# Projections with both halves of the input in one matmul, norms transposed and evicted by token tile

## The chip, the cores and the metric

The kernel runs on one core of a Trainium2 chip. The core has a matrix engine (TensorE, PE), a vector engine (VectorE, DVE), a scalar engine (ScalarE, ACT), GpSimd (POOL) and a queue engine (SyncE, SP) that issues most transfers. PE writes into PSUM, of which the kernel holds 8 banks of 128 partitions x 512 f32. The engines run their own instruction streams in order and meet by semaphores. The metric is device microseconds of one execution; the median of several runs counts.

## The reference, cut to what matters

One decoder layer for 256 tokens of width 1024, all in float32. It mixes tokens in two attention branches, then runs an expert FFN.

```
xn = rms_norm(h, norm_mix_g)
[qa ka va | qb kb vb | f_logit | g_a g_b] = xn @ w_in
ya = moba_attention(rope(qa), rope(ka), va) @ w_branch_a     # 8 heads of 64; one block: plain causal
yb = forgetting_attention(qb, kb, vb, log_sigmoid(f_logit + b)) @ w_branch_b   # 8 heads of 64
h  = h + (sigmoid(g_a) * ya + sigmoid(g_b) * yb) @ w_out
h  = h + peer_ffn(rms_norm(h, norm_ffn_g), ...)              # 8 product-key heads, top 16, 16384 experts
return rms_norm(h, norm_final_g)
```

In the forgetting attention (FoX) each score gets the difference of two cumulated logs of forget gates added: a column term for the query and a row term for the key.

## The kernel before, in words

To keep float32 accuracy every large product is made of three in a faster form: a factor is split into a high half (its value rounded to that form) and a low half (the rest), and `hi*hi + hi*lo + lo*hi` is added up in PSUM. `split` (L78) does this for a weight: SP loads a 128x1024 piece (512 KB) into one of three `raw` buffers, ACT casts the high half (L82), DVE subtracts (L83). `mm3` (L91) issues the three matmuls, L92, L95 and L96.

A projection (`proj_t`, L166) multiplies one such weight piece with the normed, transposed input `xt`: eight pieces of the contraction (`KD = 8`), three matmuls of 128x256 each, so 24. `xt1` (first norm) and `xt2` (second norm) are pairs of tiles, high and low. The first projections of a norm are "late": the 16 matmuls with the high weight come first (L176) and the 8 with the low one last (L178).

`norm_t` (L138) makes such an input. For the two token tiles it computes the scale (squares L126, root L133, reciprocal L135), scales on DVE (`xn`, L145), transposes 16 blocks on PE into four banks (L151) and evicts eight 128x256 tiles, each first on ACT (high half, L156) and then on DVE (low half, L157).

The order in the program: the first norm; the forget gate's logits (24 small matmuls) and their chain of log-sigmoid, cumulated sum and negation (L218 to L230); a small array goes to memory (`cd`) and comes back broadcast to all partitions (`crow`, L234, on POOL's queue); eight FoX projections for q and k, four value pieces (`w_va`); FoX attention woven with the eight MoBA projections, MoBA attention woven with the 16 gate projections; then branch and output projections, the second norm, 16 `w_pq` projections of the FFN, and 2 x 128 expert pieces. On each engine the framework's scheduler fixes the order when the program is built; `after` adds orders by hand. PSUM has four names (`tp`, `sp`, `py`, `mm`) of two banks each. 14 matmuls on zeros (L199) run while the input is loaded.

Of the kernel before, what the change touches and what calls it, by code (L numbers as in the profile page):

```python
# [50 lines left out]
def body(ctx, tc, x, g_mix, w_fb, w_va, w_qk, w_gate, w_f, b_f, w_br, w_out, g_ffn, w_pq,  # L51
# [24 lines left out]
    lows = []  # L76

    def split(src, behind=None):  # L78
# [3 lines left out]
        ih = nc.scalar.copy(out=h, in_=r)  # L82
        il = nc.vector.tensor_tensor(out=l, in0=r, in1=h.bitcast(F32), op=ALU.subtract)  # L83
        lows.append(il)
        if behind is not None:
            for i, b in zip((ih, il), behind):
                if b is not None:
                    after(i, b)
        return h, l

# [14 lines left out]
    xt2 = [keep.tile([P, KD, S], F32R, name=f"xt2{i}") for i in "hl"]  # L105
# [32 lines left out]
    def norm_t(pool, xin, gi, xt, tags, junk, vector=(), cuts=(512, 1024)):  # L138
        xs = []
        for t in range(NT):  # L140
            rs = norm_rstd(pool, xin[:, t], junk, vector[t] if vector else (), cuts)
            xn = pool.tile([P, D], F32, name="xn", bufs=2)
            for n in range(2):
                sl = slice(n * 512, (n + 1) * 512)
                nc.vector.tensor_scalar(out=xn[:, sl], in0=xin[:, t, sl], scalar1=rs, scalar2=None, op0=ALU.mult)  # L145
            xs.append(xn)
        pss = [bank(tag) for tag in tags]
        for t in range(NT):
            for k in range(KD):
                o = (k % 2 * NT + t) * P  # L150
                nc.tensor.transpose(pss[k // 2][:, o:o + P], xs[t][:, k * P:(k + 1) * P], ident)  # L151
        evs = []
        for k in range(KD):
            g = gm[:, gi, k:k + 1]
            src = pss[k // 2][:, k % 2 * S:(k % 2 + 1) * S]
            ia = nc.scalar.mul(out=xt[0][:, k], in_=src, mul=g)  # L156
            iv = nc.vector.scalar_tensor_tensor(  # L157
                out=xt[1][:, k], in0=src, scalar=g, in1=xt[0][:, k].bitcast(F32),
                op0=ALU.mult, op1=ALU.subtract)
            evs.append(ia)  # L160
        return ia, iv, evs[1]
# [4 lines left out]
    def proj_t(src, xt, behind=None, tag="mm", late=False):  # L166
        w = split(src, behind)
        ps = bank(tag)[:, :S]
        if not late:
            for k in range(KD):  # L170
                mm3(ps, wk(w, k), [v[:, k] for v in xt], k == 0, k == KD - 1)
        else:

            for k in range(KD):
                for v in xt:
                    nc.tensor.matmul(ps, lhsT=wk(w, k)[0], rhs=v[:, k], start=k == 0 and v is xt[0], stop=False)  # L176
            for k in range(KD):
                nc.tensor.matmul(ps, lhsT=wk(w, k)[1], rhs=xt[0][:, k], start=False, stop=k == KD - 1)  # L178
# [3 lines left out]
    with ExitStack() as fr:  # L182
# [15 lines left out]
        for _ in range(14):  # L198
# [9 lines left out]
        xt1 = [fp.tile([P, KD, S], F32R, name=f"xt1{i}") for i in "hl"]  # L208
# [5 lines left out]
        ps = bank("tp")[:HEADS, :S]  # L214
        for k in range(KD):
            mm3(ps, wk(wfs, k, HEADS), [v[:, k] for v in xt1], k == 0, k == KD - 1)
        fx = fp.tile([HEADS, S], F32, name="fx")
        nc.vector.tensor_scalar(out=fx, in0=ps, scalar1=bf, scalar2=None, op0=ALU.add)  # L218
        fa = fp.tile([HEADS, S], F32, name="fa")
        nc.scalar.activation(out=fa, in_=fx, func=AF.Abs)  # L220
        nc.scalar.activation(out=fa, in_=fa, func=AF.Exp, scale=-1.0)
        nc.scalar.activation(out=fa, in_=fa, func=AF.Ln, bias=1.0)
        lf = fp.tile([HEADS, S], F32, name="lf")
        nc.vector.scalar_tensor_tensor(out=lf, in0=fx, scalar=0.0, in1=fa, op0=ALU.min, op1=ALU.subtract)
        cf = fp.tile([HEADS, S], F32, name="cf")
        nc.vector.tensor_tensor_scan(out=cf, data0=lf, data1=lf, initial=0.0, op0=ALU.add, op1=ALU.bypass)

        cn = fp.tile([HEADS, 3 * P], F32, name="cn")
        nc.vector.tensor_scalar(out=cn[:, P:], in0=cf, scalar1=-1.0, scalar2=None, op0=ALU.mult)
        nc.vector.tensor_scalar(out=cn[:, :P], in0=cf[:, :P], scalar1=-1.0, scalar2=None, op0=ALU.mult)  # L230
        cd = drm.tile([HEADS, 3 * P], F32, name="cd")
        nc.gpsimd.dma_start(out=cd, in_=cn)
        crow = fp.tile([P, HEADS, 3, P], F32, name="crow")
        nc.gpsimd.dma_start(out=crow.rearrange("p h t k -> p (h t k)"), in_=cd.rearrange("h k -> (h k)").partition_broadcast(P))  # L234

        cq = fp.tile([P, NT, HEADS], F32, name="cq")
        tp = bank("tp")
        for t in range(NT):
            nc.tensor.transpose(tp[:, t * HEADS:(t + 1) * HEADS], cf[:, t * P:(t + 1) * P], ident[:HEADS, :HEADS])
        nc.scalar.copy(out=cq, in_=tp[:, :NT * HEADS].rearrange("p (t h) -> p t h", h=HEADS))  # L240

        mask = cmx[:, C_MASK:C_MASK + 3 * P]
        def heads_qk(br, i):
            fox = br == 0
            dst = []
            for c in range(4):
                behind = (normed1[2] if c == 0 else normed1[0], normed1[1]) if fox and i == 0 and c < FIRST else None
                ps = proj_t((w_fb if fox else w_qk)[i * 4 + c], xt1, behind, late=behind is not None, tag=("mm", "sp", "mm", "py")[c] if fox else "mm")
                q = fp.tile([P, S], F32, name=f"qk{br}{i}{c}")
                sc = 0.125 if i == 0 else 1.0  # L250
                if fox:
                    nc.scalar.mul(out=q, in_=ps, mul=sc)
                else:
                    q0 = fw.tile([P, S], F32, name="q0")
                    nc.scalar.mul(out=q0, in_=ps, mul=sc)
                    qp = [fw.tile([P, S], F32R, name=f"q0{i}") for i in "hl"]
                    nc.scalar.mul(out=qp[0], in_=ps, mul=sc)
# [11 lines left out]

        def projections(br, res):  # L270
            res.append((yield from heads_qk(br, 0)))
            res.append((yield from heads_qk(br, 1)))
            if br == 0:
# [5 lines left out]
            for c in range(4):  # L279
                w = split(w_va[br * 4 + c])  # L280
                for t in range(NT):
                    for kk in range(2):
                        k = 2 * c + kk
                        mm3(pv[t], [a[:, k, t * P:(t + 1) * P] for a in xt1], wk(w, kk, 512), k == 0, k == KD - 1)
# [5 lines left out]
        def attention(br, qs, ks, v):  # L290
# [7 lines left out]
            if fox:  # L298
                for hh in (slice(0, 4), slice(4, 8)):
                    nc.vector.tensor_tensor(out=crow[:, hh, 0::2], in0=crow[:, hh, 0::2], in1=mask[:, :P].unsqueeze(1).unsqueeze(1).to_broadcast([P, 4, 2, P]), op=ALU.add)  # L300
            for h in range(HEADS + 1):
                if h < HEADS:
# [6 lines left out]
                    if fox:  # L309
                        ch = crow[:, h].rearrange("p t k -> p (t k)")  # L310
                        for t, o, n in ((0, 0, P), (1, P, S)):
                            nc.vector.scalar_tensor_tensor(out=s[:, o:o + n], in0=sp[:, o:o + n], scalar=cq[:, t, h:h + 1], in1=ch[:, o:o + n], op0=ALU.add, op1=ALU.add)
# [67 lines left out]
        mt = [fp.tile([P, KD, S], F32R, name=f"xt1{i}") for i in "hl"]  # L380
# [25 lines left out]
        def w_out_step(k, t, n, behind=None):  # L406
            ps, lo, hi = po[t][n]
            return mm3(ps[:, :hi - lo], [a[:, k, t * P:(t + 1) * P] for a in mt], [a[:, lo:hi] for a in ws[k]], k == 0, k == KD - 1, behind)
# [8 lines left out]
        for t in range(NT):  # L417
            for n, (ps, lo, hi) in enumerate(po[t]):
                for k in range(KD - LATE, KD):
                    last = w_out_step(k, t, n, last)  # L420
                nc.vector.tensor_tensor(out=x2[:, t, lo:hi], in0=ps[:, :hi - lo], in1=xin[:, t, lo:hi], op=ALU.add)
# [363 lines left out]
```

## Time and profile before

| | |
|---|---|
| runs | 1024.62, 1026.22 (median), 1028.5 us |
| profiled execution | 1024.9 us, span 1023.1 us from first to last instruction |
| mean granted clock of PE | 0.996 of full speed |
| busy | PE 98%, weight loads 90%, DVE 73%, ACT 53%, POOL 1% of the span |
| memory | 176.88 MB read, 174 GB/s over the span |

The first 55 us hold the norm and the FoX projections, the second norm lies near 210 us, and the FFN takes the remaining 800 us; busy shares of the whole are mostly those of the FFN.

### The profile page before, as it was taken

The numbers are of one execution on the slowest core, as the hardware profiler recorded it, in microseconds if no ns is written. First come the engines' busy times: TensorE is split into PE (matmuls) and PEld (weight loads), VectorE is DVE, ScalarE is ACT, GpSimd is POOL, SyncE is SP. The second block draws the span as 40 slices with busy tenths as digits, with TensorE's granted clock in tenths as the row PEclk, the third lists the DMA queues.
The fourth block names the chain that finished last, engine by engine and source line by source line (L and its number), as shares of the span: only waits on it lengthen the run. The fifth ranks groups of instructions, "written<-read, shape, count | busy, mean of one in ns | idle before, by whom it ended". The sixth has DMA issues, their size and how long they took to land.

```text
span 1023.1 us, 18580 instructions
## 1 busy us (share of the span) xinstructions
PE 1007.5 (98%) x7068; PEld 924.6 (90%) x7068; DVE 748.6 (73%) x1603; ACT 541.9 (53%) x983; POOL 7.4 (1%) x13
## 2 busy tenths in 40 slices
PE   8999999989999999999999999999999999999997
PEld 6898999989999999999999999988888888888886
DVE  5575546679999996788888889866656666665665
ACT  6555566454554544555544444455555555555554
POOL 0000000000000000000000000000000000000001
PEclk9999999999999999999999999999999999999999
DMA  6654435655566565555555555566566666666663
GB/s 217 221 154 130 127 110 182 186 167 164 149 190 200 173 186 178 165 163 164 159 164 163 162 164 165 166 185 196 195 190 198 189 192 197 191 197 190 193 197 123
DMA packets 50040, 179.14 MB, mean 175 GB/s; under 512 B 5768, under 2 KB 6672, under 8 KB 49696
## 3 DMA queue, kind: packets, MB, share of 16 engines
q1 hardware_dynamic: 49104, 175.62, 55.9%
q0 software_dynamic: 416, 1.69, 0.5%
q8 instruction: 55, 0.90, 0.4%
q10 hardware_dynamic: 432, 0.66, 0.2%
q14 instruction: 33, 0.27, 0.1%
HBM read 176.88 MB, written 1.06 MB: 174 GB/s over the span
## 4 chain that ended last, share of the span: by engine, by line
PE 97%; DVE 1%; DMA 0%; ACT 0%; issue 0%; SPq 0%; DVEq 0%; ACTq 0%
PE mm L92 17%; PE mm L95 17%; PE mm L96 17%; PE py L92 7%; PE py L95 7%; PE py L96 7%; PE sp L96 6%; PE sp L95 6%; PE sp L92 6%; PE tp L608 3%; PE mm L176 1%; PE sp L308 1%; PE sp L577 1%; PE tp L324 1%; PE mm L178 0%; DMA xin<-in_x_dram 0%
## 5 line engine op out<-in xcount | busy, mean ns | idle before, releaser
L83 DVE TENSOR_TENSOR lo<-raw,hi 128x1024 fp32r<-128x1024 f32 x328 | 399.8, 1221 | 134.7 <-ACT hi L82 134.7
L82 ACT CAST hi<-raw 128x1024 fp32r<-128x1024 f32 x328 | 344.8, 1053 | 281.2 <-PE mm L95 181.9
L92 PE MATMUL mm<-xt2h,hi 128*128 128x256 f32 x1128 | 323.6, 287 | 0.0
L96 PE MATMUL mm<-xt2h,lo 128*128 128x256 f32 x1128 | 317.2, 281 | 0.0
L95 PE MATMUL mm<-xt2l,hi 128*128 128x256 f32 x1128 | 317.0, 281 | 0.0
L92 PEld LDWEIGHTS mm<-xt2h,hi 128*128 128x128 f32 x1128 | 212.5, 188 | 0.3
L95 PEld LDWEIGHTS mm<-xt2l,hi 128*128 128x128 f32 x1128 | 212.7, 189 | 0.0
L96 PEld LDWEIGHTS mm<-xt2h,lo 128*128 128x128 f32 x1128 | 212.5, 188 | 0.0
L645 ACT CAST ah<-act 128x256 fp32r<-128x256 f32 x128 | 52.0, 407 | 95.1 <-PE sp L95 95.1
L646 DVE TENSOR_TENSOR al<-act,ah 128x256 fp32r<-128x256 f32 x128 | 54.3, 425 | 61.5 <-PE sp L96 60.5
L95 PE MATMUL py<-lo,ah 128*128 128x512 f32 x256 | 79.8, 389 | 0.0
L92 PE MATMUL py<-hi,ah 128*128 128x512 f32 x256 | 79.7, 389 | 0.0
L96 PE MATMUL py<-hi,al 128*128 128x512 f32 x256 | 79.4, 389 | 0.0
L95 PE MATMUL sp<-lo,ah 128*128 128x512 f32 x254 | 79.0, 389 | 0.0
L92 PE MATMUL sp<-hi,ah 128*128 128x512 f32 x254 | 78.8, 389 | 0.0
L96 PE MATMUL sp<-hi,al 128*128 128x512 f32 x254 | 78.7, 389 | 0.0
L602 DVE TENSOR_TENSOR oh<-iota,slot_e 128x512 f16<-128x512 f16 x128 | 53.5, 420 | 21.8 <-PE tp L608 21.1
L92 PE MATMUL mm<-xt1h,hi 128*128 128x256 f32 x208 | 60.3, 290 | 0.0
L96 PE MATMUL mm<-xt1h,lo 128*128 128x256 f32 x208 | 59.5, 286 | 0.0
L95 PE MATMUL mm<-xt1l,hi 128*128 128x256 f32 x208 | 59.2, 285 | 0.0
L96 PEld LDWEIGHTS py<-hi,al 128*128 128x128 f32 x256 | 48.1, 188 | 10.0
L92 PEld LDWEIGHTS py<-hi,ah 128*128 128x128 f32 x256 | 48.1, 188 | 10.0
(256 smaller groups left out, 1333.6 us busy)
## 6 DMA issues: line engine op xcount, KB each, us to landing
raw<-in_u_t_dram SPq DMA_DIRECT2D x128, 512.0 KB, 3.6
raw<-in_v_e_dram SPq DMA_DIRECT2D x128, 512.0 KB, 3.6
raw<-in_w_gate_dram SPq DMA_DIRECT2D x16, 512.0 KB, 3.6
raw<-in_w_pq_dram SPq DMA_DIRECT2D x16, 512.0 KB, 3.9
raw<-in_w_fb_dram SPq DMA_DIRECT2D x8, 512.0 KB, 4.1
raw<-in_w_va_dram SPq DMA_DIRECT2D x8, 512.0 KB, 3.7
raw<-in_w_qk_dram SPq DMA_DIRECT2D x8, 512.0 KB, 3.7
raw<-in_w_br_dram SPq DMA_DIRECT2D x8, 512.0 KB, 3.6
```

What stands on the lines that cost most here:

```text
L82: ih = nc.scalar.copy(out=h, in_=r)
L83: il = nc.vector.tensor_tensor(out=l, in0=r, in1=h.bitcast(F32), op=ALU.subtract)
L92: i = nc.tensor.matmul(ps, lhsT=lhs[0], rhs=rhs[0], start=start, stop=False)
L95: nc.tensor.matmul(ps, lhsT=lhs[0], rhs=rhs[1], start=False, stop=False)
L96: return nc.tensor.matmul(ps, lhsT=lhs[1], rhs=rhs[0], start=False, stop=stop)
L176: nc.tensor.matmul(ps, lhsT=wk(w, k)[0], rhs=v[:, k], start=k == 0 and v is xt[0], stop=False)
L308: nc.tensor.matmul(sp[:, o:o + n], lhsT=q[:, t * P:(t + 1) * P], rhs=k[:, :n], start=True, stop=True)
L324: nc.tensor.transpose(tp[:, j * P:(j + 1) * P], pg[:, j * P:(j + 1) * P], ident)
L602: nc.vector.tensor_tensor(out=oh, in0=iota.unsqueeze(1).to_broadcast(wide), in1=slot_e[:, :, s2].unsqueeze(2).to_broadcast(wide), op=ALU.i ...
L608: nc.tensor.matmul(ps[:, q * NK:(q + 1) * NK], lhsT=ohs[q // 2][:, 1, :, q % 2], rhs=gis[q // 2][:, part, :, q % 2], start=part == 0, stop ...
L645: nc.scalar.copy(out=ah, in_=at(i))
L646: nc.vector.tensor_tensor(out=al, in0=at(i), in1=ah.bitcast(F32), op=ALU.subtract)
```

## The change

Four things change. First, `xt` becomes one tile in which the high and low half of a piece lie side by side, so that one matmul of 512 columns multiplies both with a high weight; `proj_w` does so for 7 FoX, 8 MoBA and 16 gate projections, and the two halves of the result are added when evicted (`both`: ACT copies one, DVE adds the other). The scale of 0.125 goes from the eviction into `split`. Second, both norms are transposed and evicted token tile by token tile, in 128x128 blocks; a tile's blocks lie in two banks. Third, the first projection of each norm starts with tile 0 (`mm2_t`), and the forget gate's matmuls stand behind its first eight. The forget chain comes after the fourth FoX projection, its broadcast array has 256 instead of 384 values a head, and its columns are transposed after the eighth projection. Fourth, there are 22 matmuls on zeros for 14. The order of the loads on SP's queue stays. The other `w_pq` projections, the expert pieces, branch and output projections stay as they were.

```diff
+    def split(src, behind=None, scale=None):
...
+            ih = nc.scalar.mul(out=h, in_=r, mul=scale)
+            il = nc.vector.scalar_tensor_tensor(out=l, in0=r, scalar=scale, in1=h.bitcast(F32), op0=ALU.mult, op1=ALU.subtract)
...
+    def mm2(ps, w, xt, then=None, ks=range(KD)):
+        for k in ks:
+            i = nc.tensor.matmul(ps, lhsT=wk(w, k)[0], rhs=xt[2][:, k], start=k == 0, stop=False)
...
+        for k in ks:
+            i = nc.tensor.matmul(ps[:, :S], lhsT=wk(w, k)[1], rhs=xt[0][:, k], start=False, stop=k == KD - 1)
+    def mm2_t(ps, w, xt, t, then=None):
+        for k in range(KD):
+            i = nc.tensor.matmul(ps[:, t * S:(t + 1) * S], lhsT=wk(w, k)[0], rhs=xt[2][:, k, :, t * P:(t + 1) * P], start=k == 0 and t == 0, stop=False)
...
+    def both(out, ps):
+        nc.scalar.copy(out=out, in_=ps[:, S:])
+        return nc.vector.tensor_tensor(out=out, in0=ps[:, :S], in1=out, op=ALU.add)
...
-    xt2 = [keep.tile([P, KD, S], F32R, name=f"xt2{i}") for i in "hl"]
+    xt2 = parts(keep.tile([P, KD, 2, S], F32R, name="xt2"))
...
-                o = (k % 2 * NT + t) * P
-                nc.tensor.transpose(pss[k // 2][:, o:o + P], xs[t][:, k * P:(k + 1) * P], ident)
+            blocks = [pss[2 * t + k % 2][:, k // 2 * P:(k // 2 + 1) * P] for k in range(KD)]
...
+                ia = nc.scalar.mul(out=xt[0][:, k, cols], in_=blocks[k], mul=g)
+                iv = nc.vector.scalar_tensor_tensor(
+                    out=xt[1][:, k, cols], in0=blocks[k], scalar=g, in1=xt[0][:, k, cols].bitcast(F32),
+                    op0=ALU.mult, op1=ALU.subtract)
...
-        for _ in range(14):
+        for _ in range(22):
...
+        w0 = split(w_fb[0], (normed1[2], normed1[1]), 0.125)
+        ps0 = bank("mm")
+        first0 = mm2_t(ps0, w0, xt1, 0)
...
+            gate_last = mm3(ps, wk(wfs, k, HEADS), [v[:, k] for v in xt1[:2]], k == 0, k == KD - 1, first0 if k == 0 else None)
...
-        crow = fp.tile([P, HEADS, 3, P], F32, name="crow")
+        crow = fp.tile([P, HEADS, S], F32, name="crow")
...
             res.append((yield from heads_qk(br, 0)))
+            if br == 0:
+                forget()
...
-                ps = proj_t(w_gate[c], xt1)
-                g = gate[:, c // KD, c % KD]
-                nc.scalar.copy(out=g, in_=ps)
+                ps = proj_w(w_gate[c], xt1)
+                both(gate[:, c // KD, c % KD], ps)
```

The first place is ACT's stream at the start of the program, from the first eviction of the first norm to the forget gate's Abs (`fa`). `hi<-raw` are high halves of weight pieces, `tp`, `sp`, `py` are banks. Before:

```order
L156 ACTIVATE xt1h<-tp,gm 128x256
L156 ACTIVATE xt1h<-sp,gm 128x256
L156 ACTIVATE xt1h<-tp,gm 128x256
L156 ACTIVATE xt1h<-py,gm 128x256
L156 ACTIVATE xt1h<-tp,gm 128x256
L82 CAST hi<-raw 128x1024
L156 ACTIVATE xt1h<-sp,gm 128x256
L156 ACTIVATE xt1h<-tp,gm 128x256
L156 ACTIVATE xt1h<-py,gm 128x256
L82 CAST hi<-raw 128x1024 x3
L220 ACTIVATE fa<-fx 8x256
```

And of the change, from the sixth block on:

```order
L206 ACTIVATE xt_130<-sp,gm 128x128
L206 ACTIVATE xt_130<-tp,gm 128x128 x2
L206 ACTIVATE xt_130<-py,gm 128x128
L206 ACTIVATE xt_130<-sp,gm 128x128
L206 ACTIVATE xt_130<-tp,gm 128x128 x2
L206 ACTIVATE xt_130<-py,gm 128x128
L206 ACTIVATE xt_130<-sp,gm 128x128
L87 ACTIVATE hi<-raw 128x1024
L206 ACTIVATE xt_130<-tp,gm 128x128
L206 ACTIVATE xt_130<-py,gm 128x128
L87 ACTIVATE hi<-raw 128x1024 x3
L322 ACTIVATE fa<-fx 8x256
```

14 evictions of 128x128, from both token tiles in turn, stand ahead of the first high half, where five of 128x256 stood.

The second place is DVE's stream around the two adds of the causal mask to `crow`. `lo<-raw,hi` are low halves, `s<-sp,cq,crow` the first scores. Before:

```order
L229 TENSOR_SCALAR cn<-cf 8x256
L230 TENSOR_SCALAR cn<-cf 8x128
L83 TENSOR_TENSOR lo<-raw,hi 128x1024 x3
L300 TENSOR_TENSOR crow<-crow,cmx 128x4x2x128 x2
L83 TENSOR_TENSOR lo<-raw,hi 128x1024 x2
L312 SCALAR_TENSOR_TENSOR s<-sp,cq,crow 128x128
```

And of the change, where L137 is the add that evicts a merged projection:

```order
L331 TENSOR_SCALAR cn<-cf 8x256
L84 TENSOR_TENSOR lo<-raw,hi 128x1024
L137 TENSOR_TENSOR qk_303<-sp,qk_303 128x256
L84 TENSOR_TENSOR lo<-raw,hi 128x1024
L137 TENSOR_TENSOR qk_329<-mm,qk_329 128x256
L84 TENSOR_TENSOR lo<-raw,hi 128x1024
L137 TENSOR_TENSOR qk_355<-py,qk_355 128x256
L379 TENSOR_TENSOR crow_600<-crow,cmx 128x1024
L380 TENSOR_TENSOR crow<-crow,cmx 128x8x128
L84 TENSOR_TENSOR lo<-raw,hi 128x1024
L137 TENSOR_TENSOR qk_393<-mm,qk_393 128x256
```

The low half behind the adds was the first value piece's; it is now that of the eighth projection, and four adds that evict projections stand behind it too.

The third place is DVE's stream in the second norm, from the statistics of the second token tile on (`rs` its reciprocal, `xn` the scaling). Before:

```order
L129 SCALAR_TENSOR_TENSOR st<-ss,st 128x1
L135 RECIPROCAL rs<-sd 128x1
L145 TENSOR_SCALAR xn<-x_80,rs 128x512 x2
L157 SCALAR_TENSOR_TENSOR xt2l<-tp,gm,xt2h 128x256
L157 SCALAR_TENSOR_TENSOR xt2l<-py,gm,xt2h 128x256
```

And of the change:

```order
L177 SCALAR_TENSOR_TENSOR st<-ss,st 128x1
L207 SCALAR_TENSOR_TENSOR xt_78<-tp,gm,xt_78 128x128
L183 RECIPROCAL rs<-sd 128x1
L207 SCALAR_TENSOR_TENSOR xt_78<-py,gm,xt_78 128x128
L193 TENSOR_SCALAR xn<-x_79,rs 128x512 x2
L207 SCALAR_TENSOR_TENSOR xt_78<-tp,gm,xt_78 128x128
```

Two evictions of tile 0 have moved ahead of the scaling of tile 1; the other 14 stand behind it.

## Rows read from the trace of the kernel before

**Rows 1.** The page, busy time and instructions; chain that ended last, share of span by engine
```profile
PE 1007.5 (98%) x7068; PEld 924.6 (90%) x7068; DVE 748.6 (73%) x1603; ACT 541.9 (53%) x983; POOL 7.4 (1%) x13
...
PE 97%; DVE 1%; DMA 0%; ACT 0%; issue 0%; SPq 0%; DVEq 0%; ACTq 0%
```

**Rows 2.** What PE waited for: us in total, times, longest
```profile
PE tp L92 <- DVE xt1l L157: 2.0, 1, 2.0
...
PE mm L95 <- DVE lo L83: 1.1, 1, 1.1
PE mm L176 <- ACT xt2h L156: 0.6, 1, 0.6
```

**Rows 3.** Timeline of PE: start us, duration us, instruction
```profile
30.39 0.28 PE L92 MATMUL sp<-xt1h,hi 128*128 128x256 f32 x1
...
33.27 0.28 PE L92 MATMUL mm<-xt1h,hi 128*128 128x256 f32 x1
...
45.28 0.39 PE L92 MATMUL mm<-hi,xt1h 128*128 128x512 f32 x1
...
45.96 0.39 PE L92 MATMUL mm<-hi,xt1h 128*128 128x512 f32 x1
```

**Rows 4.** Groups by line and form: busy us, mean ns of one | idle before
```profile
L319 ACT ACTIVATE pe<-s,nm 128x256 f32<-128x256 f32 x16 | 8.0, 498 | 0.0
...
L319 ACT ACTIVATE pe<-s,nm 128x128 f32<-128x128 f32 x16 | 6.4, 403 | 4.4 <-DVE nm L318 4.3
...
L258 DVE TENSOR_TENSOR q0l<-q,q0h 128x256 fp32r<-128x256 f32 x8 | 3.3, 418 | 0.0
```

**Rows 5.** Busy us of PE, PEld, DVE, ACT, POOL in a stretch; granted clock, DMA share, GB/s
```profile
60.00:80.00 20.00, 20.00 (x172) 19.54 (x171) 15.91 (x36) 12.47 (x32) 0.00 (x0) 1.00 0.46 136
```

**Rows 6.** Timeline of all engines, start of the program
```profile
1.23 4.63 PE L199 MATMUL py<-wz 128*128 128x512 f16 x14 [1.23 <-DVE wz L196]
...
7.94 0.88 DVE L145 TENSOR_SCALAR xn<-xin,rs 128x512 f32<-128x512 f32 x2
...
8.96 0.47 ACT L156 ACTIVATE xt1h<-tp,gm 128x256 fp32r<-128x256 f32 x1 [1.25 <-PE tp L151]
...
9.33 0.47 ACT L156 ACTIVATE xt1h<-sp,gm 128x256 fp32r<-128x256 f32 x1
...
10.76 1.07 ACT L82 CAST hi<-raw 128x1024 fp32r<-128x1024 f32 x1
...
11.57 0.38 PE L92 MATMUL tp<-xt1h,wfh 128*8 128x256 f32 x1 [1.99 <-DVE xt1l L157]
...
18.55 1.05 ACT L82 CAST hi<-raw 128x1024 fp32r<-128x1024 f32 x1 [3.74 <-DMA raw<-in_w_fb_dram]
```

**Rows 7.** Half-microsecond stretches, columns as in group 5
```profile
11.00:11.50 0.50, 0.00 (x0) 0.00 (x0) 0.50 (x2) 0.50 (x1) 0.00 (x0) 0.50 0.75 284
...
14.50:15.00 0.50, 0.50 (x7) 0.41 (x6) 0.50 (x2) 0.31 (x1) 0.00 (x0) 1.00 0.00 0
...
219.50:220.00 0.50, 0.50 (x7) 0.50 (x6) 0.50 (x1) 0.00 (x0) 0.00 (x0) 1.00 0.73 205
```

**Rows 8.** Timeline, second norm
```profile
213.03 0.47 ACT L156 ACTIVATE xt2h<-tp,gm 128x256 fp32r<-128x256 f32 x1 [1.25 <-PE tp L151]
...
218.27 0.41 PE L176 MATMUL mm<-xt2l,hi 128*128 128x256 f32 x1
...
218.48 0.41 PE L176 MATMUL mm<-xt2h,hi 128*128 128x256 f32 x1
```

**Rows 9.** The forget bias: its DMA (KB, us to landing); timelines of DVE and PE
```profile
crow<-cd POOLq DMA_DIRECT2D x1, 1536.0 KB, 10.2
...
38.63 2.36 DVE L300 TENSOR_TENSOR crow<-crow,cmx 128x1024 f32<-128x1024 f32 x2 [5.86 <-DMA crow<-cd]
...
40.55 0.49 PE L92 MATMUL mm<-hi,xt1h 128*128 128x512 f32 x1 [0.27 <-ACT qk L252]
42.18 0.50 PE L95 MATMUL mm<-lo,xt1h 128*128 128x512 f32 x1 [1.14 <-DVE lo L83]
```

More of the change, by code (lines that the diff above doesn't have):

```diff
@@ L74, in load @@
         return r
-    lows = []
-    def split(src, behind=None):
+    lows, highs, ends = [], [], []
+    def split(src, behind=None, scale=None):
         r = load(src)
@@ L144, in norm_t, with proj_w, proj_t @@
                 sl = slice(n * 512, (n + 1) * 512)
[L145 removed]
+                i = nc.vector.tensor_scalar(out=xn[:, sl], in0=xin[:, t, sl], scalar1=rs, scalar2=None, op0=ALU.mult)
+                if t == 0 and n == 1 and ahead is not None:
+                    after(i, ahead)
             xs.append(xn)
         pss = [bank(tag) for tag in tags]
+        evs = []
         for t in range(NT):
+            cols = slice(t * P, (t + 1) * P)
+            blocks = [pss[2 * t + k % 2][:, k // 2 * P:(k // 2 + 1) * P] for k in range(KD)]
             for k in range(KD):
[L150 to L161 removed]
+                nc.tensor.transpose(blocks[k], xs[t][:, k * P:(k + 1) * P], ident)
+            for k in range(KD):
+                g = gm[:, gi, k:k + 1]
+                ia = nc.scalar.mul(out=xt[0][:, k, cols], in_=blocks[k], mul=g)
+                iv = nc.vector.scalar_tensor_tensor(
+                    out=xt[1][:, k, cols], in0=blocks[k], scalar=g, in1=xt[0][:, k, cols].bitcast(F32),
+                    op0=ALU.mult, op1=ALU.subtract)
+                evs.append(ia)
+        return ia, iv, evs[KD - 1]
     def wk(w, k, n=P):
         return [v[:, k * n:(k + 1) * n] for v in w]
[L166 removed]
+    def proj_w(src, xt, behind=None, tag="mm", scale=None, then=None):
+        w = split(src, behind, scale)
+        ps = bank(tag)
+        ends.append(mm2(ps, w, xt, then))
+        return ps
+    def proj_t(src, xt, behind=None, tag="mm", late=False, then=None):
         w = split(src, behind)
@@ L170, in proj_t @@
             for k in range(KD):
-                mm3(ps, wk(w, k), [v[:, k] for v in xt], k == 0, k == KD - 1)
+                i = mm3(ps, wk(w, k), [v[:, k] for v in xt[:2]], k == 0, k == KD - 1)
         else:
             for k in range(KD):
-                for v in xt:
-                    nc.tensor.matmul(ps, lhsT=wk(w, k)[0], rhs=v[:, k], start=k == 0 and v is xt[0], stop=False)
+                for v in xt[:2]:
+                    i = nc.tensor.matmul(ps, lhsT=wk(w, k)[0], rhs=v[:, k], start=k == 0 and v is xt[0], stop=False)
+                    if then is not None:
+                        after(i, then)
             for k in range(KD):
-                nc.tensor.matmul(ps, lhsT=wk(w, k)[1], rhs=xt[0][:, k], start=False, stop=k == KD - 1)
+                i = nc.tensor.matmul(ps, lhsT=wk(w, k)[1], rhs=xt[0][:, k], start=False, stop=k == KD - 1)
+        ends.append(i)
         return ps
@@ L571, in body @@
             first = m < FIRST
-            ps = proj_t(w_pq[m], xt2, (None if m == 0 else normed[0], normed[1]) if first else (qhs[m - FIRST], None), late=first)
             qh = tw.tile([P, S], F32, name="qh")
-            qhs.append(nc.scalar.copy(out=qh, in_=ps))
+            if m == 0:
+                w = split(w_pq[m], (None, normed[1]))
+                ps = bank("mm")
+                for t in range(NT):
+                    mm2_t(ps, w, xt2, t)
+                mm2_l(ps, w, xt2)
+                qhs.append(both_t(qh, ps))
+            else:
+                ps = proj_t(w_pq[m], xt2, (normed[0], normed[1]) if first else (qhs[m - FIRST], None), late=first)
+                qhs.append(nc.scalar.copy(out=qh, in_=ps))
             sp = bank("sp")[:, :NT * NK]
```

116 lines of the change are left out of this document (75 added, 41 removed).

## The prediction

> **What bounds the kernel now.** I read the shares and the chain of waits first. TensorE (PE) is busy for 1007.5 of 1023.1 us, and 97% of the chain that ended last is PE itself [rows 1]. So an edit counts for what it does to PE's queue: fewer or shorter matmuls, or a changed wait. What PE waits for is in the list of its waits, and the lines that this change touches are few there: 2.0 us for the last-needed eviction of the first norm, 1.1 us for one low half of a weight, 0.6 us in the second norm [rows 2]. I therefore price the change in two ways: matmuls by their pitch (start to start), and three places (start, FoX bias, second norm) by following the engines through them in the timeline.
>
> The pitch comes from the timeline of PE [rows 3]. One projection of 24 matmuls of 128x256 runs from 30.39 to 33.27 us, 0.120 us each. Three matmuls with 512 columns run from 45.28 to 45.96, 0.227 us each. So 512 columns cost 0.013 us less than twice 256. That is all that merging a pair can give.
>
> **The merged projections.** 31 projections replace 16 matmuls of 256 columns by 8 of 512; the other 8 stay. Each saves 8 x (2 x 0.120 - 0.227) = 0.107 us. The 7 of FoX give 0.75 us, the 8 of MoBA and the 16 gates 2.55 us. The bounds are nothing (if a merged matmul costs by its columns alone) and the full 3.3 us; I take the full, since the row is the same instruction shape on the same kind of operand.
>
> The Trainium skill ("TensorE: Matmul & The Clock Gate", section Back-to-back issue gap) gives about 131 ns sustained for N=512 with a weight load to each matmul. The row here has 227 ns in just such a stream, so the trace doesn't agree.
>
> Each merged projection needs its two halves added: ScalarE (ACT) copies one as it did before, and VectorE (DVE) gets a new add. The nearest row is the existing 128x256 add at 418 ns [rows 4]. In the stretch of MoBA projections DVE is busy for 15.9 of 20 us beside a PE that is busy throughout [rows 5]. Six chunks (of 2.88 us, with attention between them) fall into 20 us there, so the adds bring 2.5 us, to 18.4 of 20. I cost them at nothing because a projection's bank is wanted again only two projections (5.5 us) later. Without that cover they would cost their own time, 24 x 0.42 = 10 us, which is the far bound. The scale of 0.125 moves from the eviction into the split and adds no instruction.
>
> **The start.** Before, ACT evicts five 128x256 tiles, makes the high half of the first weight at 10.76, and PE begins at 11.57 with the forget gate's matmuls, which need no projection weight [rows 6]. Afterwards the first matmuls are the projection's, so PE needs tile 0 and that high half, and in ACT's order 14 small evictions stand ahead of it. What does a small one cost? Large ones start 0.37 us apart on ACT (8.96, 9.33) [rows 6]. The same operation at 128x128 is 0.095 us shorter than at 128x256 [rows 4]. So I take 0.27 us. ACT's third eviction reads the bank that DVE's first one must have read, and DVE is on the second tile's scaling until 7.94 + 0.88 = 8.82 us [rows 6]. From there 14 x 0.27 = 3.8 us, and 1.05 us of the cast, give a first matmul at 13.75: **+2.2 us**. If ACT isn't held, it begins near 7.8, behind the dummies and tile 0's first transposes, and the figure is +1.1; if a small eviction is no cheaper than a large one, it is +3.4.
>
> The rule that speaks against this order is in the Trainium skill ("PSUM — Partial Sum Buffer", section PSUM bank collisions raise a hardware error): reads of one bank by ACT and DVE must be ordered too. A tile's eight blocks lie in two banks here, so the engines take turns. The trace of before can't tell it from the plain need for ACT's result: there DVE follows ACT in any case.
>
> The eight extra dummy matmuls are free if they end before the first transposes have their data. The 14 now take 4.63 us and end at 5.86 [rows 6]; eight more at the pitch of 512 columns, 0.23 us [rows 3], end near 7.7, which delays tile 0's transposes by half a microsecond. Tile 1's can't begin before its scaling, at 7.94, has written a half [rows 6], and DVE's evictions stand behind that scaling anyway. I cost them at nothing.
>
> PE's granted clock drops to 0.50 (the lower level, 1.2 GHz; 1.00 is 2.4) at 11.0 us after two idle microseconds [rows 2] and is back at 14.5 [rows 7]. A matmul at that level takes 0.21 us (218.27 to 218.48 [rows 8]), 0.093 more. I assume the same number of slow matmuls as now.
>
> **The FoX bias.** The broadcast of the forget bias moves 1536 KB in 10.2 us, and its adds begin the moment it lands, 38.63; behind them in DVE's order stand two low halves, and PE sits idle for 0.27 us and then 1.14 us [rows 9]; with the tails of the matmuls ahead of these gaps (0.4 to 0.5 us long at a pitch of 0.23) this costs about 1.85 us now. The gate chain starts behind the high half of the fourth weight as it does now (that cast waits for its load at 18.55 [rows 6]), so I leave the issue near 28.5. The transfer has two thirds of the bytes: 6.8 us if it goes by bytes, 10.2 if by something else. I take 7.3, so it lands at 35.8, and the adds end at 38.1. But in DVE's order they now stand one projection earlier, ahead of the eighth weight's low half and of four adds that free PE's banks. That low half then ends at 39.3, and PE, which comes to it at 39.1 (a start 2.2 us late, less 0.75), waits little; the chain of adds and halves behind it costs some 0.5 us more. I take a stall of 0.55 for 1.85: **-1.3 us**.
>
> **The second norm.** Tile 0's first ACT eviction now stands ahead of tile 1's square root, and two DVE evictions ahead of tile 1's scaling. Each is worth 0.3 us, so tile 1 is scaled 0.6 to 0.75 us later. PE may in exchange finish half of chunk 0 early. Chunk 1's matmuls start at 218.48 now, when ACT's first eviction is at 213.03 [rows 8]. DVE's 14 remaining evictions go in pairs, and three of the pairs reuse the banks of the pair ahead and wait for ACT; that ends near 218.2, so chunk 1 starts at 218.65: **+0.2 us**, between -0.5 (banks never waited for) and +1.5 (each pair waits).
>
> **Sum.** +2.2 - 0.75 - 1.3 - 2.55 + 0.2 = -2.2 us. The profiled execution took 1024.9 us (span 1023.1 and 1.8 around it), 1.3 below the median of 1026.22, so it goes to 1022.7 and the median to **1024.0**. Its three runs spread by 4 us; 0.5% (5.1 us: 1021.1 to 1031.4) is about what a measurement can tell from no change.
>
> **The rivals.**
> - *The clock stays low* (the other side). PE is now interrupted for longer and then works in pieces behind evictions. If all 48 matmuls at the start and 48 at the second norm run at 0.21 us, that is 35 and 31 more slow ones than now, 3.3 and 2.9 us, less 0.5 that the bias's slack takes up: 1029.7. It turns the sign from 24 extra slow matmuls on (2.2 / 0.093). For it: an idle stretch of two microseconds was enough for the fall [rows 7], and the new one is four. Against it: once PE had work in an unbroken row the clock came back both times [rows 7]. 0.11.
> - *The bias's transfer still takes 10.2 us.* It lands at 38.65, the eighth low half at 42.2, 2.9 us after PE wants it: 1026.9. For it: 128 partitions read one and the same small source, which needn't go by bytes. 0.12.
> - *DVE can't hide its adds.* It works in order and would be 92% busy beside PE [rows 5]; if a quarter of the 10 us shows, 1026.5. 0.13.
> - *The start isn't late and the clock stays up*, through the dummies: 1.1 less for the start and 13 slow matmuls (1.2 us) fewer: 1021.7. 0.13.
> - *Merged matmuls cost their columns alone:* 3.3 us are gone, 1027.3. 0.02. By the skill's 131 ns the 248 merged matmuls would save 248 x (0.240 - 0.131) = 27 us, about 999; with 227 ns in the rows I give it 0.01.
>
> **How the numbers follow.** My forecast keeps 0.48: 1024.0, on its own from 1022 to 1026. From 1019.8 to 1029.5 it takes in all but the far ends of the first and fourth rivals. Faster by over 0.5% (below 1021.1) holds part of the fourth, the 0.01, and an execution that falls well: 0.11. Slower by over 0.5% needs the low clock and one more rival: 0.04. The rest, 0.85, is no change.
>
> **What would show it.** Merged matmuls 0.227 us apart and PE's projections of 2.78 us for 2.88; a first real matmul near 13.75; the bias's transfer near 7 us and PE's gap at 39 to 42 us down to half a microsecond; no PE wait for DVE's adds in the MoBA stage; chunk 1 of the second norm within half a microsecond of where it is, against the end of the output projection. I am wrong if the start is late by more than 3.4 us, if low clock lasts past a whole projection, or if a wait for the new adds appears among PE's waits.

## The result and the profile after

| | before | after |
|---|---|---|
| median of 20 runs | 1024.83 us | 1031.55 us |
| range | 1023.84 to 1028.5 | 1027.96 to 1033.81 |
| ratio | | 1.0052, interval 1.0043 to 1.0061 |
| profiled execution, span | 1024.9, 1023.1 us | 1032.01, 1030.2 us |
| mean granted clock of PE | 0.996 | 0.992 |

The change makes the kernel 0.5% slower. The forecast was 1024.0, with a range up to 1029.5; the time lies outside it and on the other side of before. The forecast was built on 1026.22, the median of three runs of the kernel before; 20 runs have 1024.83. So it is the change that has to be compared: -2.2 us forecast, +6.7 by the medians, +7.1 by the profiled executions. Eight of the 20 runs after took 1028.0 to 1029.6 us at mean clocks of 0.993 to 0.998 and twelve 1030.8 to 1033.8 at 0.991 to 0.994; the profiled one is of the twelve, and no trace shows why the eight were shorter.

Where the 7.1 us of the profiled execution went is seen when the same piece of work on PE is followed through both timelines. Each line is a start in one trace less the start of its counterpart in the other:

```
PE instruction                                       before     after     lag
first matmul with real weights                        11.57     13.41    +1.84
first matmul of the eighth FoX projection             36.15     37.48    +1.33
first matmul of the value pieces                      39.02     44.10    +5.08
first MoBA projection                                 54.78     60.31    +5.53
first branch projection                              161.89    167.74    +5.85
last matmul of the output projection                 209.37    215.08    +5.71
a low-half matmul of the first w_pq chunks           226.20    232.62    +6.42
last matmul                                         1016.20   1023.32    +7.12
```

Nearly 4 us are lost between the eighth projection and the value pieces. The list of PE's waits in the kernel after names the place (us in total, times, longest):

```profile
PE mm L114 <- ACT hi L87: 3.9, 1, 3.9
PE py L108 <- DVE lo L84: 2.3, 1, 2.3
...
PE mm L114 <- DVE xt L207: 1.0, 2, 0.7
...
PE mm L140 <- ACT act L671: 0.2, 1, 0.2
```

The first row is the late start (where [rows 2] had 2.0 us), the second is new. The start, in ACT's timeline after:

```profile
9.09 0.75 ACT L206 ACTIVATE xt<-tp,gm 128x128 fp32r<-128x128 f32 x2 [0.16 <-DVE xt L207]
...
12.23 1.13 ACT L87 ACTIVATE hi<-raw 128x1024 fp32r<-128x1024 f32 x1
```

The timeline of PE after shows what stands around both waits:

```profile
13.41 1.43 PE L114 MATMUL mm<-xt,hi 128*128 128x256 f32 x8 [3.88 <-ACT hi L87]
...
31.89 2.00 PE L104 MATMUL sp<-xt,hi 128*128 128x512 f32 x8
33.73 1.11 PE L108 MATMUL sp<-xt,lo 128*128 128x256 f32 x8
34.69 2.00 PE L104 MATMUL mm<-xt,hi 128*128 128x512 f32 x8
...
37.48 2.00 PE L104 MATMUL py<-xt,hi 128*128 128x512 f32 x8
41.78 2.08 PE L108 MATMUL py<-xt,lo 128*128 128x256 f32 x8 [2.30 <-DVE lo L84]
43.79 0.38 PE L339 MATMUL tp<-cst,cf 8*128 8x8 f32 x2
44.10 0.80 PE L140 MATMUL mm<-hi,xt 128*128 128x512 f32 x1
```

Two things are to be seen. A merged projection takes 1.84 us for eight matmuls of 512 columns (31.89 to 33.73, 0.230 each) and 0.96 for eight of 256: 2.80 us for the 2.88 of [rows 3]. And PE idles for 2.3 us ahead of the eighth projection's second half, which then takes 2.01 us to the next instruction for the 0.96 of its neighbours. DVE's timeline after tells why it is late:

```profile
38.23 1.23 DVE L379 TENSOR_TENSOR crow<-crow,cmx 128x1024 f32<-128x1024 f32 x1 [7.24 <-DMA crow<-cd]
39.38 1.22 DVE L380 TENSOR_TENSOR crow<-crow,cmx 128x1024 f32<-128x1024 f32 x1
40.51 1.22 DVE L84 TENSOR_TENSOR lo<-raw,hi 128x1024 fp32r<-128x1024 f32 x1
41.65 0.42 DVE L137 TENSOR_TENSOR qk<-mm,qk 128x256 f32<-128x256 f32 x1
```

DVE sits for 7.24 us on the bias's transfer, and the low half that PE needs stands behind it. The transfer has two thirds of its bytes and is hardly faster (KB, us to landing; 10.2 in [rows 9]):

```profile
crow<-cd POOLq DMA_DIRECT2D x1, 1024.0 KB, 9.5
```

Why PE is then slow, the stretches show (busy us of PE, PEld, DVE, ACT, POOL; granted clock, DMA share, GB/s):

```profile
39.00:41.00 2.00, 0.48 (x3) 0.06 (x1) 2.00 (x3) 2.00 (x4) 0.00 (x0) 1.00 0.03 10
41.00:43.00 2.00, 1.22 (x5) 1.22 (x6) 2.00 (x3) 0.04 (x1) 0.00 (x0) 0.64 0.04 16
43.00:45.00 2.00, 2.00 (x9) 1.66 (x8) 1.99 (x4) 0.00 (x0) 0.00 (x0) 0.50 0.80 287
45.00:47.00 2.00, 2.00 (x6) 1.34 (x5) 0.58 (x1) 1.39 (x3) 0.00 (x0) 0.50 0.90 262
47.00:49.00 2.00, 2.00 (x7) 1.28 (x6) 0.98 (x2) 0.00 (x0) 0.00 (x0) 0.66 0.85 272
```

Two microseconds without work, and the granted clock is at 0.50, 1.2 GHz, just when the work comes. It stays there from 41.5 to 48.3 us. PE has work in 6.5 us of that, and half of it, 3.3 us, is lost on top of the wait. In the kernel before PE idled in the same place, but in two pieces with work between them [rows 9], and the clock was at 1.00 there. In its trace:

```profile
41.00:43.00 2.00, 0.86 (x5) 0.69 (x5) 2.00 (x2) 1.98 (x3) 0.00 (x0) 1.00 0.01 4
```

In the second norm, the timeline of DVE after shows the two evictions ahead of tile 1's scaling, as the order had it:

```profile
217.66 0.35 DVE L207 SCALAR_TENSOR_TENSOR xt<-tp,gm,xt 128x128 fp32r<-128x128 f32 x1 [0.43 <-ACT xt L206]
217.93 0.15 DVE L183 RECIPROCAL rs<-sd 128x1 f32<-128x1 f32 x1
218.10 0.35 DVE L207 SCALAR_TENSOR_TENSOR xt<-py,gm,xt 128x128 fp32r<-128x128 f32 x1
218.37 0.87 DVE L193 TENSOR_SCALAR xn<-x,rs 128x512 f32<-128x512 f32 x2
```

### The profile page after: what moved, and what is told of

Same layout as the page of the kernel before. It is cut to its first block, busy times and chain, and to the rows that moved or that the text cites. A ratio compares the mean times of both kernels' runs of the same rounds, so it can differ in the third digit from the quotient of the medians.

```text
span 1030.2 us, 18171 instructions
## 1 busy us (share of the span) xinstructions
PE 1013.8 (98%) x6828; PEld 915.1 (89%) x6828; DVE 761.8 (74%) x1651; ACT 545.3 (53%) x999; POOL 7.5 (1%) x13
## 3 DMA queue, kind: packets, MB, share of 16 engines
HBM read 176.36 MB, written 1.06 MB: 172 GB/s over the span
## 4 chain that ended last, share of the span: by engine, by line
PE 74%; DVE 3%; ACT 1%; issue 0%; ACTq 0%
PE mm L140 12%; PE mm L143 12%; PE mm L144 12%; PE py L144 6%; PE py L143 6%; PE py L140 6%; PE sp L140 6%; PE sp L144 6%; PE sp L143 6%; PE tp L694 3%; DVE lo L84 1%; PE sp L663 1%; PE mm L232 0%; DVE idx L542 0%; DVE idx L538 0%; ACT hi L83 0%
## 5 line engine op out<-in xcount | busy, mean ns | idle before, releaser
L83 ACT CAST hi<-raw 128x1024 fp32r<-128x1024 f32 x320 | 336.5, 1052 | 287.6 <-PE mm L143 154.7
L84 DVE TENSOR_TENSOR lo<-raw,hi 128x1024 fp32r<-128x1024 f32 x320 | 390.6, 1221 | 127.8 <-ACT hi L83 126.4
L140 PE MATMUL mm<-xt,hi 128*128 128x256 f32 x1128 | 323.8, 287 | 0.2 <-ACT act L671 0.2
L144 PE MATMUL mm<-xt,lo 128*128 128x256 f32 x1128 | 317.2, 281 | 0.0
L143 PE MATMUL mm<-xt,hi 128*128 128x256 f32 x1128 | 317.0, 281 | 0.0
L140 PEld LDWEIGHTS mm<-xt,hi 128*128 128x128 f32 x1128 | 212.5, 188 | 0.8 <-ACT act L671 0.6
L143 PEld LDWEIGHTS mm<-xt,hi 128*128 128x128 f32 x1128 | 212.7, 189 | 0.0
L144 PEld LDWEIGHTS mm<-xt,lo 128*128 128x128 f32 x1128 | 212.4, 188 | 0.0
L143 PEld LDWEIGHTS py<-lo,ah 128*128 128x128 f32 x256 | 48.1, 188 | 10.0
L144 PEld LDWEIGHTS sp<-hi,al 128*128 128x128 f32 x254 | 47.7, 188 | 9.9
L143 PEld LDWEIGHTS sp<-lo,ah 128*128 128x128 f32 x254 | 47.7, 188 | 9.9
```

Of the source, the lines that this page charges most:

```text
L140: i = nc.tensor.matmul(ps, lhsT=lhs[0], rhs=rhs[0], start=start, stop=False)
L143: nc.tensor.matmul(ps, lhsT=lhs[0], rhs=rhs[1], start=False, stop=False)
L144: return nc.tensor.matmul(ps, lhsT=lhs[1], rhs=rhs[0], start=False, stop=stop)
```

## The experiments

Of the names, "the first experiment" is the one with the bias's adds later. All ratios are to the kernel before; the lags quoted are those of PE behind before, found as above. In the diffs a minus line is the changed kernel's, for those that start from the kernel before its own.

**The bias's adds two low halves later.** Only DVE's order changes (`mark` holds the low half of the second value piece).

```diff
-                nc.vector.tensor_tensor(out=crow0, in0=crow[:, :, :P], in1=tri, op=ALU.add)
-                nc.vector.tensor_tensor(out=crow[:, :, P:], in0=crow[:, :, P:], in1=tri, op=ALU.add)
+                for i in (nc.vector.tensor_tensor(out=crow0, in0=crow[:, :, :P], in1=tri, op=ALU.add),
+                          nc.vector.tensor_tensor(out=crow[:, :, P:], in0=crow[:, :, P:], in1=tri, op=ALU.add)):
+                    after(i, mark[0])
```

> The changed kernel with one edit: the two mask adds on the forget bias stand two low halves later in DVE's order. Theory A (the adds wait for the bias's transfer with the eighth low half behind them; PE idles 2.3 us for it and then runs 6.8 us at the lower clock, 3.4 us lost): the PE wait for that low half goes below 0.3 us, the low clock between 41 and 48 us is gone, and the time falls by 5 to 6 us, to 1026 to 1027. Theory B (the late start, the adds in the MoBA stage and the second norm are the cause): the time falls by less than 2 us.

1026.79 us, ratio 1.0006 (0.9993 to 1.0019): 4.7 us of the loss of 5.3 (0.0046 x 1025) are gone. The same stretches in this kernel:

```profile
39.00:41.00 2.00, 2.00 (x15) 1.70 (x13) 1.27 (x2) 2.00 (x4) 0.00 (x0) 1.00 0.08 29
41.00:43.00 2.00, 2.00 (x10) 1.42 (x9) 2.00 (x3) 1.98 (x5) 0.00 (x0) 1.00 0.56 94
43.00:45.00 2.00, 2.00 (x12) 1.38 (x12) 2.00 (x4) 0.78 (x1) 0.00 (x0) 1.00 0.85 272
45.00:47.00 2.00, 2.00 (x12) 1.41 (x9) 2.00 (x5) 0.00 (x0) 0.00 (x0) 1.00 0.42 166
```

PE is never idle and the clock stays at 1.00. Theory A holds. The late start is still there (first matmul 13.79 us, a lag of 2.2); ahead of the second norm the merge, and the waits that only the kernel before has at 40 to 42 us, have brought the lag down to 0.3 us, and it is 1.3 at the end. In this trace the clock didn't fall at the second norm at all, though it did in both kernels before and after.

**Matmuls on zeros in the gap.** DVE's order and the transfer stay as in the changed kernel; ten matmuls that nobody reads keep PE at work while it waits.

```diff
+        if fill is not None:
+            fill(i)
         for k in ks:
             i = nc.tensor.matmul(ps[:, :S], lhsT=wk(w, k)[1], rhs=xt[0][:, k], start=False, stop=k == KD - 1)
...
+        def busy(behind):
+            zps = bank("tp")
+            for _ in range(10):
+                i = nc.tensor.matmul(zps, lhsT=wz[:, :P], rhs=wz, start=True, stop=True)
+                after(i, behind)
+            ends.append(i)
```

> The changed kernel with ten matmuls on zeros between the high and the low half of the eighth projection, where PE idles 2.3 us; DVE's order and every wait stay. If the wait costs its own length and, through the clock that falls in it, another 3.4 us: the stretch at the lower clock from 41 to 48 us is gone, and the time falls by about 3 us to 1028 to 1028.7. If the lower clock comes from something else than the idle PE, or costs nothing: within 1 us of the changed kernel.

1028.68 us, ratio 1.0022 (1.0011 to 1.0034): 3.1 us faster than the changed kernel (0.0030 x 1025). The stretches after the gap, in this kernel:

```profile
41.00:43.00 2.00, 2.00 (x12) 0.94 (x11) 2.00 (x4) 1.01 (x2) 0.00 (x0) 1.00 0.01 4
43.00:45.00 2.00, 2.00 (x15) 1.74 (x14) 2.00 (x4) 0.00 (x0) 0.00 (x0) 1.00 0.58 180
```

The low half comes no earlier for it, but the clock is at 1.00 when the real work resumes. So of the 4.7 us, about 3 were the clock and under 2 the wait itself.

**Half of the bias's bytes.** Four of eight heads are left out, with zeros in their place; the base is the first experiment.

```diff
-            nc.gpsimd.dma_start(out=crow.rearrange("p h k -> p (h k)"), in_=cd.rearrange("h k -> (h k)").partition_broadcast(P))
+            nc.gpsimd.dma_start(out=crow[:, :4].rearrange("p h k -> p (h k)"), in_=cd[:4].rearrange("h k -> (h k)").partition_broadcast(P))
+            nc.gpsimd.memset(crow[:, 4:], 0.0)
```

> The first experiment's kernel with half of the forget bias left out: four of eight heads are broadcast (512 KB), zeros stand for the other four. If the transfer goes by its own bytes: 9.2 us become 4.6 to 5. If its time is set by something else than its bytes (its share of the DMA engines beside the weight loads): 7 us or more. The time of the whole doesn't count here.

In this kernel the transfer shows as:

```profile
crow<-cd POOLq DMA_DIRECT2D x1, 512.0 KB, 7.1
```

So it doesn't go by its own bytes alone. Over all traces 1536 KB took 9.0 to 10.2 us, 1024 KB 7.0 to 9.5, 512 KB 7.1. That the weight loads, which share the DMA engines with it (0.8 busy, 273 GB/s, in the kernel after between 28.7 and 38.2 us), set its time is what I think, but no run takes them away.

**The merge alone,** put into the kernel before with 8 FoX, 8 MoBA and 16 gate projections; all edits are those of the diff above.

> The kernel before with the merged projections alone (8 FoX, 8 MoBA, 16 gates, their DVE adds, the scale in the split); norms, start and forget chain as before. If the merge pays by the pitch of the changed kernel (0.230 us for 512 columns, 0.120 for 256, so 0.08 us a projection): 32 x 0.08 = 2.6 us faster, 1022.3. If DVE's adds or banks eat it in the MoBA stage: within 1 us of before. If the scheduler puts the bias's adds ahead of the eighth low half here too: slower by 2 us or more.

1024.2 us, ratio 0.9976 (0.9964 to 0.9988): 2.5 us by the ratio, 1.4 by the medians; the lag is -1.2 us where the second norm starts, and -0.8 at the end. Here the adds on the bias stand behind the eighth low half.

**The gates' merge alone,** on the kernel before:

```diff
-                ps = proj_t(w_gate[c], xt1)
-                g = gate[:, c // KD, c % KD]
-                nc.scalar.copy(out=g, in_=ps)
+                both(gate[:, c // KD, c % KD], proj_w(w_gate[c], xt1))
```

> The kernel before with the 16 gate projections merged, nothing else. If a merge is worth what the pitches say (8 x (2 x 0.120 - 0.230) = 0.08 us): 1.3 us of PE's time, so 0.9 to 1.5 us faster, and more than half of the gain of all 32 merged projections. If the merge of all gained little because DVE's adds hold the MoBA stage: the gates alone gain as much as all 32 or more.

1023.47 us, ratio 0.9980 (0.9966 to 0.9994): by the intervals the 16 give as much as all 32.

**The MoBA projections' merge alone,** on the kernel before:

```diff
-                    nc.scalar.mul(out=q0, in_=ps, mul=sc)
+                    both(q0, ps)
...
-                    nc.scalar.mul(out=qp[0], in_=ps, mul=sc)
+                    nc.scalar.copy(out=qp[0], in_=q0)
```

> The kernel before with the eight MoBA projections merged, nothing else. By the pitches (0.08 us a projection) 0.65 us faster. If the added DVE adds and the longer chain from the projection to its rotation hold PE in that stage: equal to before or slower, although the merged matmuls keep their pitch. All 32 merged gave 1.4 to 2.4 us, the 16 gates alone about as much.

1027.94 us, ratio 1.0015 (1.0001 to 1.0030): slower, though the interval only just says so. What the stage costs is seen when the time from each PE start to the next is summed by kind, from the first MoBA projection to the first branch projection (us; the changed kernel has the scores of 13 heads in the stage, the others those of 12; a head is four of the trace's matmuls):

```
kernel          projections  values  scores  transposes  probabilities x values  rotation  stage
before                69.59   11.33    8.70        5.15                    9.90      2.44  107.11
gates merged          67.51   11.33    7.64        6.00                    9.90      2.44  104.82
MoBA merged           68.74   11.62    9.75        5.46                   10.13      2.32  108.01
changed kernel        67.22   11.89    9.75        6.28                    9.84      2.45  107.43
```

The line of the projections falls by 2.4 us in the changed kernel, 2.1 for the gates, 0.85 for MoBA. Not all of that is the merge. Behind another projection's matmul the next start comes after 0.120 us at 256 columns and 0.231 at 512, in each of these traces that has them, so a merged projection saves 8 x (0.240 - 0.231) = 0.07 us: 1.7 us for the 23 of the changed kernel in the stage, 1.1 for the 15 gates, 0.6 for MoBA. Most of the rest is a matter of where time is booked: a projection's matmul right behind a transpose is booked with 0.20 us and the transpose with 0.03, and there are 23 such places before, 8 in the changed kernel.

With MoBA merged, the small matmuls woven between the projections cost 1.8 us more (39.28 for 37.52), though their number is the same and PE waits for nothing in the stage. The scheduler puts them into another order with the new adds, and for the scores the traces tell what the order costs. Two rows of the kernel before:

```profile
53.93 0.92 PE L308 MATMUL sp<-qk,qk 64*128 64x128 f32 x4
54.78 0.39 PE L92 MATMUL mm<-xt1h,hi 128*128 128x256 f32 x1
...
60.73 0.93 PE L308 MATMUL sp<-qk,qk 64*128 64x128 f32 x8
61.59 0.38 PE L261 MATMUL tp<-q0h,rot 128*128 128x256 f32 x1
```

One head's four matmuls hold PE for 0.85 us up to the next start, and two heads' eight in one row for 0.86: the second head is free. With the gates merged there are three such rows of eight in the stage and one more pair of heads that partly overlaps, in the kernel before one and two, with MoBA merged one and none. That makes up the 1.06 us by which the scores are cheaper with the gates merged, and most of the 1.05 by which they are dearer with MoBA merged. So the gates gained 2.3 us in the stage, of which 1.1 is the merge, and MoBA lost 0.9 although the merge gave 0.6. In the changed kernel, less the 0.85 us of the 13th head, the stage is 0.5 us shorter for the 1.7 that the merge gives there. What the values and transposes lose in the new orders is not taken apart here.

**The start as before** (evictions of 128x256, gate's matmuls first, 14 matmuls on zeros), on the first experiment. The edit puts the old lines of the diff above back.

```diff
-        for _ in range(22):
+        for _ in range(14):
...
-        normed1 = norm_t(fw, xin, 0, xt1, ("tp", "sp", "tp", "py"), "mm", ((0,), ()))
+        normed1 = norm_w(fw, xin, 0, xt1, ("tp", "sp", "tp", "py"), "mm", ((0,), ()))
...
-        w0 = split(w_fb[0], (normed1[2], normed1[1]), 0.125)
-        ps0 = bank("mm")
-        first0 = mm2_t(ps0, w0, xt1, 0)
-        ps = bank("py")[:HEADS, :S]
+        ps = bank("tp")[:HEADS, :S]
```

> The first experiment's kernel with the first norm, the first projection and the gate's matmuls as before (evictions of 128x256, gate first, 14 dummies). PE starts 1.84 us later in the changed kernel and is 1.33 us late at the eighth projection after a gain of 0.6 us by the merge: this kernel should be 1.8 us faster than the first experiment if the start stands on the path to the end, and equal to it if a later wait takes the time up.

1023.41 us, ratio 0.9970 (0.9957 to 0.9983): 3.7 us faster than the first experiment by the ratios, 2.6 by the lag at the end, so the start stands on the path to the end, with at least its late first matmul (lags 2.23 and -0.07).

**Tile 0's evictions ahead of tile 1's,** on the first experiment, with the first high half behind ACT's fifth eviction:

```diff
+                if t > 0 and apart:
+                    after(ia, evs[KD - 1])
+                    after(iv, ivs[KD - 1])
...
-        return ia, iv, evs[KD - 1]
+        return ia, iv, evs[KD - 4] if apart else evs[KD - 1]
```

> The first experiment's kernel (bias adds later) with the order of the first norm's evictions set: all eight of tile 0 ahead of those of tile 1 on ACT and on DVE, and the first weight's high half behind ACT's fifth. If the late start comes from the two tiles' evictions taking turns ahead of that high half: PE's first projection matmul at about 12.0 us instead of 13.4, and 1 us or more faster than the first experiment. If tile 0's two banks make ACT and DVE take turns at 0.44 us a block: the first matmul comes no earlier than 12.5 and tile 1 ends later, so that the time is equal to the first experiment's or longer.

1026.36 us, ratio 1.0003 (0.9990 to 1.0015): the same as the first experiment. Its timeline, PE and ACT:

```profile
11.71 2.04 PE L114 MATMUL mm<-xt,hi 128*128 128x256 f32 x8 [1.95 <-ACT hi L87]
```

```profile
10.61 1.04 ACT L87 ACTIVATE hi<-raw 128x1024 fp32r<-128x1024 f32 x1
...
12.33 0.37 ACT L206 ACTIVATE xt<-sp,gm 128x128 fp32r<-128x128 f32 x1 [0.16 <-DVE xt L207]
...
14.95 0.37 ACT L206 ACTIVATE xt<-tp,gm 128x128 fp32r<-128x128 f32 x1 [0.16 <-DVE xt L207]
15.22 0.36 ACT L206 ACTIVATE xt<-py,gm 128x128 fp32r<-128x128 f32 x1
```

Both theories were half right. PE starts at 11.71, so the order of the evictions had made the start late; but a tile's two banks make ACT wait for DVE at every second block, and tile 1's last block leaves ACT at 15.6 us instead of 14.3. That is the order of reads that the Trainium skill asks for ("PSUM — Partial Sum Buffer", section PSUM bank collisions raise a hardware error); these rows show its price. The lag is -0.8 us ahead of the second norm for +0.3 in the first experiment; it is 0.1 for 1.3 at the end. The medians don't show that microsecond.

**The second norm as before,** on the first experiment (`norm_w` again, and `proj_t` for the first w_pq chunk).

> The first experiment's kernel with the second norm and its first projection as before (evictions of 128x256, no token-tile start). If token tiles cost the second norm what the lag of PE shows across it (0.7 us, and 0.67 more in the FFN): 0.7 to 1.4 us faster than the first experiment. If they cost nothing: equal to it within 0.5 us.

1026.52 us, ratio 1.0000 (0.9987 to 1.0012), 0.3 us below the first experiment: inconclusive, since the intervals overlap.

**The second norm by token tile alone,** on the kernel before (`norm_t`, `mm2_t` and `mm2_l` of the diff for that norm).

> The kernel before with the second norm transposed and evicted token tile by token tile, its first projection begun with tile 0, and nothing else. If that costs what PE's lag shows behind it in the changed kernel (0.7 us across the norm, 0.67 in the FFN): slower by 0.7 to 1.4 us. If the kernels that keep it lose nothing by it: within 0.7 us of before.

1026.16 us, ratio 1.0000 (0.9986 to 1.0014). The lag in the trace goes from -1.1 to +0.4 us across the norm, so it costs 1.5 us in this execution. The -1.1 ahead of it has nothing to do with the edit: DVE's order around the bias is that of the kernel before, but the transfer took 9.0 us for 10.2 in this execution,

```profile
crow<-cd POOLq DMA_DIRECT2D x1, 1536.0 KB, 9.0
```

and the wait for a low half [rows 2] is gone with it. So that lead can't explain why the medians are equal; whether the norm by token tile costs anything stays open. In the first experiment's trace, where the clock didn't fall there, the lag is 0.3 us on both sides of the norm.

**Everything useful together.** Merged projections, the small bias with its adds later, both norms and the start as before (the edits of three experiments above):

> Merged projections, the small forget bias and its adds two low halves later; both norms and the start as before. If token tiles cost the start 1.8 us and the second norm 0.5 us or more: the fastest of all, 1022.5 to 1023.5, against 1023.4 with the second norm by token tile. If the second norm by token tile is worth something: slower than that by 0.5 us or more.

1022.28 us (seven runs, where the others have twelve), ratio 0.9961 (0.9943 to 0.9979): the lowest median, better than both kernels, though the interval overlaps that of the start as before. And the same with MoBA unmerged:

> Seventh experiment's kernel (both norms and start as before, small forget bias, its adds two low halves later) with the MoBA projections left unmerged, FoX and gates merged. If the merge of MoBA costs what it gives: equal to the seventh experiment, 1022.3, within 0.7 us. If it costs more: faster, 1021 to 1021.6. If it pays: slower by 0.7 us.

1023.14 us, ratio 0.9971 (0.9957 to 0.9985): not to be told from it. In the traces their stages differ by 0.1 us (106.52 and 106.41, 11 heads each): what MoBA's merge lost alone is not lost in every order.

## Why the prediction was wrong, point by point

- **The step that failed is the FoX bias.** It was -1.3 us and measured about +4 (lag from +1.33 to +5.53). Of the 9.3 us between the -2.2 forecast and the +7.1 measured, this term has 5.5, the merge behind it 2.9, the FFN 0.7 and the second norm 0.5. Three parts of it were wrong. The transfer took 9.5 us for the 7.3 taken, and 7.3 had no row behind it; the wait for the eighth low half was 2.3 us for 0.55 in all; and the fall of the clock in that wait, some 3.3 us, stood in no term. The order of the instructions was read rightly: this low half behind the adds is just where PE waits. The runs with the adds later and with matmuls on zeros show the wait and the clock apart.
- **The rival of the slow transfer** had the right mechanism, at 0.12, and the wrong price: 2.9 us and no word of the clock. My rival of the low clock was placed at the start and the second norm, where the clock fell for as long as before (3.4 us each), not where the change made a new idle stretch. Put together they would have ended beyond 1030 (1026.9 and 3.3). The prediction gave the low clock with one more rival 0.04, as if the two came by separate chances; here the one brought the other.
- **The start** was right: first matmul 13.41 for the 13.75 forecast, small evictions 0.25 to 0.27 us apart, held by DVE behind its scaling (8.70 us). That it came so near is in part luck: only 12 of the 14 evictions stood behind the hold, which ended at 9.09 us and not at 8.82, and the forecast's own sum (8.82 + 3.8 + 1.05) gives 13.67.
- **The merge** was right in direction and too large: 0.230 us for 0.227 in FoX, so 0.08 us a projection for 0.107, and 0.07 in the stage behind. FoX gave about 0.5 us by the eighth projection. MoBA and gates gave 1.7 us in their matmuls for the 2.55 forecast, and the order of the woven work took most of that; the lag went from +5.53 to +5.85, with one head's scores left over in the stage. I had looked for DVE's adds in PE's waits; there they are not. The rule of the Trainium skill weighed there ("TensorE: Matmul & The Clock Gate", section Back-to-back issue gap: 131 ns sustained at 512 columns) is off for this stream: the rows after show 230 ns too.
- **The second norm** was +0.7 for +0.2, within the bounds given; it is one execution's figure.
- **The FFN,** which had no term, adds 0.7 us between 279 and 319 us. DVE is busy there for 39.85 of 40 us from 280 on (39.83 before), and PE once waits 0.2 us for an activation. That DVE's work behind the second norm decides there, so that what PE gains or loses ahead of it isn't handed on one to one, fits this but is not shown.

## What to carry to other kernels

Before an instruction that waits for a transfer is moved up in an in-order queue, list what is now behind it, and take the transfer's old duration for the price, not its bytes, unless a run shows that it goes by them. A new idle stretch on PE costs its length and then, if the clock falls in it, half of the low stretch behind it: here 2 us brought 3 more. A merge that saves some hundredths of a microsecond at each projection also makes the scheduler order the small matmuls anew, and here that moved the stage by as much either way: look at the rows between the merged ones before calling one merge good and another bad.

## What the runs showed of the hardware

- The granted clock fell in an idle stretch of PE of 2.3 us, and not where PE idled for 0.27 and 1.14 us with work between. About two idle microseconds don't always bring the fall: at the start, PE idled for 1.99 us in the kernel before and for 2.00 in the last kernel above (MoBA unmerged), and in the second trace the clock stayed at 1.00. At the second norm it stayed low for 3.4 us in the kernel before, for 6.8 with both norms and the start as before, and didn't fall at all in three traces (the first experiment, the start as before on it, tile 0 ahead). So a lag between two single executions can hold this difference too; those three traces, with 3.4 us at the start each, can be compared with one another.
- Four score matmuls of 64 rows held PE for 0.85 us, and eight of two heads in one row for 0.86.
- A broadcast from memory to 128 partitions took 7.1 us at 512 KB and 7.0 to 9.5 at 1024 KB, 9.0 to 10.2 at 1536 KB.
- 128x128 evictions from PSUM start 0.25 us apart on ACT and 0.26 on DVE if the banks alternate, and 0.37 a block on average where one tile's two banks make the engines take turns (12.60 to 15.22 on ACT with tile 0 ahead).
